# SSD state update by two 256-column vector operations instead of four of 64, and xe taken from the transposed x in PSUM

## The chip, the cores and the metric

The kernel runs on one core of a Trainium2 chip. The metric is the device time of one execution in microseconds (us), as the median of several runs. The core has five engines with a queue each: TensorE (PE, with its weight loads shown as PEld), VectorE (DVE), ScalarE (ACT), GpSimd (POOL) and SyncE (SP), which here issues the transfers. Each queue is worked off in order; an instruction that waits for a semaphore holds what stands behind it on its engine.

## The reference

One layer of a decoder trunk: a Mamba-2 SSD branch and an attention branch read the same normalised input, are projected, gated, merged and added to the residual. Only the SSD branch matters here. For 16 heads of 64 columns, in two groups of 8 heads that share B and C (state size 64), in 8 chunks of 128 tokens:

```python
xdt = xs.astype(jnp.float32) * dt[..., None]
...
a_cs = jnp.cumsum(ac, axis=-1)
...
decay_states = jnp.exp(a_cs[..., -1:] - a_cs)
states = jnp.einsum("bclgn,bgrcl,bclgrp->bcgrpn", bc, decay_states, xc)
...
new_states = jnp.einsum("bgrzc,bcgrpn->bzgrpn", decay_chunk, states)
...
y_off = jnp.einsum("bclgn,bcgrpn,bgrcl->bclgrp", cc, prev_states, jnp.exp(a_cs))
y = (y_diag + y_off).reshape(bsz, s, g, r, p) + d_skip...
```

So the state after a chunk is the state before it, times one decay per head, plus B^T (decay_states * dt * x). The kernel runs this as a recurrence over the chunks.

## The kernel before, in words

All large products are made of a high and a low part in a reduced-precision fp32 (`split`, L97 to L100: ACT copies the high part, DVE subtracts to get the low part; all such copies stand at L98 and all such subtractions at L99, and are told apart by their tiles).

Up to about 490 us the kernel computes the input projections. In that part `ssm_sums` (L401) makes, once for all heads and chunks, the 128x128 tables `acs` (cumulated a), `dec` (decay_states, by an exponential on ACT at L418) and `ed` (the decay of a whole chunk per head, 64 rows for each of the two groups, L420 and L421); `dt` was made before it.

From about 495 to 723 us runs the SSD stage. The loop at L764 goes over four quads of heads (`qd`, four heads or 256 columns each); each quad is done in two halves of four chunks by `ssd_half` (L678). Quads 0 and 1 belong to group 0 and keep their state `st32` in partitions 0 to 63, quads 2 and 3 belong to group 1 and keep it in partitions 64 to 127. For one chunk:

- `ab` is loaded by SP (L688), made into the decay matrix on ACT (L690, L692), multiplied with `cb` on DVE (L693) and split into `m4` (m in the profile).
- PE transposes x into the PSUM tile `xps` (L698; `xp` in the profile), of which there is one buffer. DVE makes xd = x * dt (L707) from it, then xe = xd * dec (L710), both 128x256, and both are split into `xr`. Chunk 7 makes no xe.
- PE forms the state's addition `sps` (L718, three products) from the split xe. DVE brings `st32` up to date in four operations of 64 columns, one per head (L724), each st * ed + sps with ed as a scalar per partition. That is done in chunks 1 to 6 of each quad, 24 times in all; chunk 0 only copies (L720). The new state is split into `sn` on ACT and DVE (L728), with the low part in the other half of the partitions.
- PE forms `yd` (L735) and, from the previous state, `yo` (L746, L747); DVE puts them together into `ys` (L748 on 128 partitions, L751 twice on 64, for the lower and then the upper half).

Between the quads stand other projections as filling for PE (`FILL`: three value slabs by `t_slab`, L136 to L138, and seven q or k slabs by `c_slab`, L111 to L113). A scheduler in the build sets the order of the instructions on each engine; `ssd_half` gets a higher priority than the filling. After the last quad the squares `sacc` are summed by PE (L791) and DVE reads the sum (L794); the attention stage begins behind that, since it takes over the memory of this stage.

Of the kernel before, what the change touches and what calls it, by code (L numbers as in the profile page):

```python
# [27 lines left out]
ALU = mybir.AluOpType  # L28
# [37 lines left out]
def build(ctx, tc, t):  # L66
    nc = tc.nc
    V, A, G, PE, SP = nc.vector, nc.scalar, nc.gpsimd, nc.tensor, nc.sync
# [10 lines left out]
    def ev(name):  # L79
        return evp.tile([P, 1028], F32, tag="ev", bufs=4, name=name)  # L80
# [119 lines left out]
    with tc.tile_pool(name="st", bufs=1, side="right") as st, \  # L200
# [29 lines left out]
        for g in range(4, 8):  # L230
# [10 lines left out]
                        op0=ALU.mult)  # L241
        V.tensor_scalar(out=cols[:, R_SCALE:R_SCALE + 8], in0=cols[:, R_SCALE:R_SCALE + 8], scalar1=1.0, scalar2=None,
                        op0=ALU.add)
# [83 lines left out]
    dt = const.tile([P, NC, SH], F32, name="dt")  # L327
    acs = const.tile([P, NC, SH], F32, name="acs")
    dec = const.tile([P, NC, SH], F32, name="dec")
    ed = const.tile([P, NC, 8], F32, name="ed")  # L330
# [29 lines left out]
    with tc.tile_pool(name="pa", bufs=1, side="right") as pa, \  # L360
# [40 lines left out]
        def ssm_sums():  # L401
            a = ev("a")
            A.activation(out=hb[:, 24:40], in_=hb[:, 24:40], func=AF.Exp)
            V.scalar_tensor_tensor(out=a[:, 0:128].rearrange("p (c h) -> p c h", h=16), in0=dt, scalar=-1.0,
                                   in1=hb[:, 24:40].rearrange("p (o n) -> p o n", o=1).broadcast_to([P, 8, 16]),
                                   op0=ALU.mult, op1=ALU.mult)
            af = a[:, 0:128]
            ps = pap.tile([P, 512], F32, tag="pp", bufs=5, name="pp")
            PE.matmul(ps[:, 0:128], lhsT=tri, rhs=af, start=True, stop=True)
            PE.matmul(ps[:, 128:256], lhsT=ones, rhs=af, start=True, stop=True)  # L410
            PE.matmul(ps[:, 256:384], lhsT=af, rhs=tri, start=True, stop=True)
            acf = acs.rearrange("p c h -> p (c h)")
            V.tensor_copy(out=acf, in_=ps[:, 0:128])
            et = a[:, 128:256]
            A.activation(out=et, in_=ps[:, 128:256], func=AF.Exp)
            dm = a[:, 256:384]
            V.tensor_tensor(out=dm, in0=ps[:, 128:256], in1=acf, op=ALU.subtract)
            A.activation(out=dec.rearrange("p c h -> p (c h)"), in_=dm, func=AF.Exp)  # L418
            ev3 = et.rearrange("p (c h) -> p c h", h=16)
            V.tensor_copy(out=ed[0:64], in_=ev3[0:64, :, 0:8])  # L420
            V.tensor_copy(out=ed[64:128], in_=ev3[64:128, :, 8:16])  # L421
            at_ = a[:, 384:512]
            V.tensor_copy(out=at_, in_=ps[:, 256:384])
            SP.dma_start(out=a_scr, in_=at_)
            ea = a[:, 512:640]
            A.activation(out=ea, in_=ps[:, 256:384], func=AF.Exp)
            SP.dma_start(out=e_scr, in_=ea)
# [209 lines left out]
    with tc.tile_pool(name="sd", bufs=1, side="right") as sd, \  # L637
            tc.tile_pool(name="sdp", bufs=1, space=PSUM) as sdp:

        def sp():  # L640
            return sdp.tile([P, 512], F32, tag="sp", bufs=4, name="sp")
# [36 lines left out]
        def ssd_half(qd, hf, xs, ys, st32, sn):  # L678

            g = qd // 2  # L680
            gs = slice(g * 64, (g + 1) * 64)
            for c in range(4 * hf, 4 * hf + 4):
# [13 lines left out]
                xps = sdp.tile([P, 512], F32, tag="xp", bufs=1, name="xp")  # L696
# [4 lines left out]
                def h4(ap):  # L701
                    return ap.rearrange("p (h d) -> p h d", h=4)

                def hb4(src):
                    return src[:, c, 4 * qd:4 * qd + 4].rearrange("p (h o) -> p h o", o=1).broadcast_to([P, 4, 64])
                xd = sd.tile([P, 256], F32, tag="xd", bufs=2, name="xd")
                V.tensor_tensor(out=h4(xd), in0=h4(xps[:, 0:256]), in1=hb4(dt), op=ALU.mult)  # L707
                if c < NC - 1:
                    xe = sd.tile([P, 256], F32, tag="xe", bufs=2, name="xe")
                    V.tensor_tensor(out=h4(xe), in0=h4(xd), in1=hb4(dec), op=ALU.mult)  # L710
                    split(xe, xr[:, 2], xr[:, 3], 256)
                split(xd, xr[:, 0], xr[:, 1], 256, V)

# [1 line left out]
                if c < NC - 1:  # L715
                    sps = sp()
                    for n, (x, y) in enumerate(((0, 2), (1, 2), (0, 3))):
                        PE.matmul(sps[:, 0:256], lhsT=bt[:, c, x, :], rhs=xr[:, y, :], start=(n == 0), stop=(n == 2))  # L718
                    if c == 0:
                        V.tensor_copy(out=st32[gs], in_=sps[gs, 0:256])  # L720
                    else:
                        for i in range(4):
                            hq = slice(i * 64, (i + 1) * 64)
                            V.scalar_tensor_tensor(out=st32[gs, hq], in0=st32[gs, hq],  # L724
                                                   scalar=ed[gs, c, 4 * (qd % 2) + i:4 * (qd % 2) + i + 1],
                                                   in1=sps[gs, hq], op0=ALU.mult, op1=ALU.add)
                    sn = sd.tile([P, 256], F32R, tag="sn", bufs=2, name="sn")
                    split(st32[gs], sn[gs], sn[half[1 - g]], 256)  # L728

                yd = sp()  # L730
                for i in range(4):
                    o = yd[0:64, (i % 2) * 256 + (i // 2) * P:(i % 2) * 256 + (i // 2) * P + P]
# [4 lines left out]
                if c > 0:  # L737
# [6 lines left out]
                    for i in range(2):  # L744
# [4 lines left out]
                                    op=ALU.mult)  # L749
# [14 lines left out]
        for qd in range(4):  # L764
            st32, sn = sd.tile([P, 256], F32, tag="st32", bufs=1, name="st32"), None
# [487 lines left out]
```

## Time and profile before

| | |
|---|---|
| median of 3 runs | 1218.62 us (1217.94 to 1220.36) |
| the profiled execution's own time | 1224.31 us |
| its span in the trace | 1222.6 us |
| mean granted TensorE clock | 0.988 |
| busy share of the span: PE, PEld, DVE, ACT, POOL | 95%, 80%, 78%, 52%, 7% |
| DVE instructions | 1946 |
| SSD stage | about 495 to 723 us |

A busy share counts the time in which at least one instruction of the engine runs. Instructions of an engine overlap: a matmul's record lasts longer than the distance to the start of the next one, and so does many a vector operation's. What one more instruction costs is therefore the distance from start to start, and not the duration of its record. A wait row names who waited for whom, with total, number of times and the longest.

### The profile page before, as it was taken

How to read it: one execution, taken by the hardware profiler on the slowest of the kernel's cores; microseconds unless marked ns; L12 is line 12 of the kernel's file. 1: busy time of each engine (PE TensorE's matmuls, PEld its weight loads, DVE VectorE, ACT ScalarE, POOL GpSimd, SP SyncE). 2: the span in 40 equal slices, each digit the busy share in tenths (PEclk: the TensorE clock that was granted, in tenths of full speed). 3: DMA queues.
4: the chain of work that ended last, by engine and by line, in shares of the span. 5: the costliest groups of instructions: out<-in, count | busy, mean ns of one | idle time of the engine just before them, and what ended most of it. 6: DMA issues, size and time to landing. Idle time of an engine off the chain costs nothing.

```text
span 1222.6 us, 18382 instructions
## 1 busy us (share of the span) xinstructions
PE 1165.0 (95%) x6206; PEld 981.2 (80%) x6206; DVE 955.9 (78%) x1946; ACT 635.5 (52%) x1260; POOL 88.4 (7%) x152
## 2 busy tenths in 40 slices
PE   3999999999999999999999989999988999999997
PEld 2788888788877877998887778888877887788876
DVE  5856699788987784589999986664677977989967
ACT  7554443454443334776676633454456554454465
POOL 1000000000000000000000012222322220000001
PEclk9999999999999999999999989999998999999999
DMA  9665643655485676546545668422246526875334
GB/s 370 263 243 166 218 138 100 207 204 176 156 290 171 218 239 201 186 152 222 186 154 178 207 216 286 144 94 81 87 165 203 175 88 228 283 241 181 109 95 147
DMA packets 109018, 228.26 MB, mean 187 GB/s; under 512 B 12362, under 2 KB 20220, under 8 KB 107900
## 3 DMA queue, kind: packets, MB, share of 16 engines
q1 hardware_dynamic: 108924, 227.09, 55.2%
q8 instruction: 49, 0.80, 0.3%
q14 instruction: 45, 0.37, 0.1%
HBM read 159.14 MB, written 67.90 MB: 186 GB/s over the span
## 4 chain that ended last, share of the span: by engine, by line
PE 62%; DVE 16%; DMA 13%; ACT 4%; issue 4%; SPq 1%; POOL 0%; POOLq 0%; DVEq 0%; ACTq 0%
PE pp L497 4%; PE pv L1067 4%; PE pp L499 4%; PE pp L500 4%; PE lg L1036 3%; PE mm L497 3%; PE mm L499 3%; PE mm L500 3%; PE mm L112 3%; PE mm L113 3%; PE mm L111 3%; PE tp L1057 2%; DMA ab<-a_scr 2%; DMA wr<-w_c 2%; PE mm L919 2%
## 5 line engine op out<-in xcount | busy, mean ns | idle before, releaser
L98 ACT CAST wh<-wr 128x512 fp32r<-128x512 f32 (+1 forms) x214 | 131.0, 620 | 176.2 <-DMA wr<-w_c 32.4
L99 DVE TENSOR_TENSOR wl<-wr,wh 128x512 fp32r<-128x512 f32 (+1 forms) x214 | 146.9, 693 | 44.0 <-ACT wh L98 43.3
L112 PE MATMUL mm<-hl,wh 128*128 128x512 f32 x288 | 116.7, 405 | 0.4 <-DVE hl L306 0.4
L111 PE MATMUL mm<-hh,wh 128*128 128x512 f32 x288 | 116.2, 408 | 0.0
L113 PE MATMUL mm<-hh,wl 128*128 128x512 f32 x288 | 115.5, 402 | 0.0
L136 PE MATMUL mm<-wh,hh 128*128 128x256 f32 (+1 forms) x256 | 73.7, 289 | 1.9 <-DVE tmp L348 1.9
L137 PE MATMUL mm<-wl,hh 128*128 128x256 f32 (+1 forms) x256 | 74.4, 291 | 0.0
L138 PE MATMUL mm<-wh,hl 128*128 128x256 f32 (+1 forms) x256 | 73.7, 289 | 0.0
L1042 ACT ACTIVATE pr<-pr,sm 128x1024 f32<-128x1024 f32 (+3 forms) x64 | 49.9, 780 | 42.4 <-DVE sm L1041 35.1
L1060 ACT CAST pth<-tp 128x512 fp32r<-128x512 f32 (+1 forms) x80 | 42.4, 543 | 47.7 <-PE tp L1057 39.5
L1037 DVE CUSTOM_DVE_ANT_0 pr<-lg,fb 128x512 f32<-128x512 f32 (+1 forms) x96 | 51.4, 552 | 17.0 <-PE lg L1036 12.4
L112 PEld LDWEIGHTS mm<-hl,wh 128*128 128x128 f32 x288 | 55.2, 192 | 11.0 <-DVE hl L306 1.0
L113 PEld LDWEIGHTS mm<-hh,wl 128*128 128x128 f32 x288 | 55.0, 191 | 10.4
L111 PEld LDWEIGHTS mm<-hh,wh 128*128 128x128 f32 x288 | 54.7, 193 | 10.2 <-ACT hh L305 0.3
L690 ACT ACTIVATE ab<-ab,acs 128x128 f32<-128x128 f32 x128 | 41.2, 391 | 40.7 <-DMA ab<-a_scr 40.5
L1045 POOL TENSOR_SCALAR pr<-pr,sm 128x1024 f32<-128x1024 f32 (+3 forms) x64 | 51.8, 811 | 87.5 <-DVE sm L1044 70.2
L1061 DVE TENSOR_TENSOR ptl<-tp,pth 128x512 fp32r<-128x512 f32 (+1 forms) x80 | 50.0, 632 | 10.3 <-ACT pth L1060 10.2
L98 ACT CAST sh<-sr 128x512 fp32r<-128x512 f32 x57 | 34.0, 619 | 43.8 <-DVE sr L479 32.4
L796 POOL TENSOR_TENSOR fl<-fl,mhalf 128x8 f32<-128x8 f32 x1 | 1.6, 1647 | 698.2 <-DVE fl L794 698.2
L136 PEld LDWEIGHTS mm<-wh,hh 128*128 128x128 f32 x256 | 48.8, 191 | 2.4 <-DVE tmp L348 2.2
L1067 PE MATMUL pv<-pth,vh 128*128 128x256 f32 (+1 forms) x160 | 45.8, 287 | 4.5 <-DVE zg L1070 3.8
L138 PEld LDWEIGHTS mm<-wh,hl 128*128 128x128 f32 x256 | 49.1, 192 | 0.0
(407 smaller groups left out, 3509.8 us busy)
## 6 DMA issues: line engine op xcount, KB each, us to landing
wr<-w_c SPq DMA_DIRECT2D x116, 256.0 KB, 3.9
wa<-w_ada SPq DMA_DIRECT2D x8, 1024.0 KB, 11.4
g_scr<-gt SPq DMA_DIRECT2D x16, 512.0 KB, 4.2
ab<-a_scr SPq DMA_DIRECT2D x32, 256.0 KB, 3.9
gt<-g_scr SPq DMA_DIRECT2D x32, 256.0 KB, 3.7
wr<-w_ps SPq DMA_DIRECT2D x28, 256.0 KB, 2.6
wr<-w_pa SPq DMA_DIRECT2D x28, 256.0 KB, 2.8
wr<-so SPq DMA_DIRECT2D x28, 256.0 KB, 2.7
```

What stands on the lines that cost most here:

```text
L98: A.copy(out=hi[:, :n], in_=raw[:, :n])
L99: eng.tensor_tensor(out=lo[:, :n], in0=raw[:, :n], in1=f32(hi[:, :n]), op=ALU.subtract)
L111: PE.matmul(ps, lhsT=hi[:, cs], rhs=xh[k][:, hs], start=(k == 0), stop=False)
L112: PE.matmul(ps, lhsT=hi[:, cs], rhs=xl[k][:, hs], start=False, stop=False)
L113: PE.matmul(ps, lhsT=lo[:, cs], rhs=xh[k][:, hs], start=False, stop=(k == 7))
L136: PE.matmul(o, lhsT=xh[k][:, ts], rhs=hi[:, cs], start=(k == 0), stop=False)
L137: PE.matmul(o, lhsT=xh[k][:, ts], rhs=lo[:, cs], start=False, stop=False)
L138: PE.matmul(o, lhsT=xl[k][:, ts], rhs=hi[:, cs], start=False, stop=(k == 7))
L497: PE.matmul(ps, lhsT=f[0][:, w], rhs=xh[:, hs], start=(first and k == 0), stop=False, skip_group_check=True)
L499: PE.matmul(ps, lhsT=f[0][:, w], rhs=xl[:, hs], start=False, stop=False, skip_group_check=True)
L500: PE.matmul(ps, lhsT=f[1][:, w], rhs=xh[:, hs], start=False, stop=(k == 3), skip_group_check=True)
L1067: PE.matmul(pv[:, o0:256], lhsT=x[kb // 4][:, kb % 4, vs], rhs=y[:, d:d + m], start=(kb == 0 and i == 0), stop=(kb == 2 * qq + 1 and i == 2))
```

## The change

`ssm_sums` multiplies `dec` by `dt` once (one more 128x128 operation on DVE, between projections). xe is then x * (dec * dt), read from `xps`, and not from xd. The state is multiplied in place by its four decays in one operation of 256 columns, with `ed` broadcast over the 64 columns of each head, and `sps` is added in a second one. The lines behind the first insertion move by one, so that xd stands at L708, xe at L711, the multiplication at L724 and the addition at L726; from L727 on the numbers are those of before.

```diff
             A.activation(out=dec.rearrange("p c h -> p (c h)"), in_=dm, func=AF.Exp)
+            V.tensor_tensor(out=dec, in0=dec, in1=dt, op=ALU.mult)
...
                 if c < NC - 1:
                     xe = sd.tile([P, 256], F32, tag="xe", bufs=2, name="xe")
-                    V.tensor_tensor(out=h4(xe), in0=h4(xd), in1=hb4(dec), op=ALU.mult)
+                    V.tensor_tensor(out=h4(xe), in0=h4(xps[:, 0:256]), in1=hb4(dec), op=ALU.mult)
                     split(xe, xr[:, 2], xr[:, 3], 256)
...
-                        for i in range(4):
-                            hq = slice(i * 64, (i + 1) * 64)
-                            V.scalar_tensor_tensor(out=st32[gs, hq], in0=st32[gs, hq],
-                                                   scalar=ed[gs, c, 4 * (qd % 2) + i:4 * (qd % 2) + i + 1],
-                                                   in1=sps[gs, hq], op0=ALU.mult, op1=ALU.add)
+                        eh = ed[gs, c, 4 * (qd % 2):4 * (qd % 2) + 4].rearrange("p (h o) -> p h o", o=1)
+                        V.tensor_tensor(out=h4(st32[gs]), in0=h4(st32[gs]), in1=eh.broadcast_to([64, 4, 64]),
+                                        op=ALU.mult)
+                        V.tensor_tensor(out=st32[gs], in0=sps[gs, 0:256], in1=st32[gs], op=ALU.add)
```

The scheduler lays the queues of the SSD stage anew. On DVE at the start of quad 0, from the copy of chunk 0's state on (st is the state, sn its split, xr the split of xe and xd, m the split of the decay matrix), the order before is:

```order
L720 COPY st_4650<-sp 64x256
L99 TENSOR_TENSOR sn<-st_4650,sn 64x256
L724 SCALAR_TENSOR_TENSOR st_4650<-st_4650,ed,sp 64x64 x4
L99 TENSOR_TENSOR xr<-xe,xr 128x256
L99 TENSOR_TENSOR xr<-xd,xr 128x256
L99 TENSOR_TENSOR m_4818<-ab,m_4818 128x512
L707 TENSOR_TENSOR xd<-xp,dt 128x256
L748 TENSOR_TENSOR ys<-sp,eb 128x2x128
L710 TENSOR_TENSOR xe<-xd,dec 128x256
```

At the same place of the changed kernel stands:

```order
L721 COPY st_4651<-sp 64x256
L99 TENSOR_TENSOR sn<-st_4651,sn 64x256
L724 TENSOR_TENSOR st_4651<-st_4651,ed 64x256
L99 TENSOR_TENSOR xr<-xe,xr 128x256
L726 TENSOR_TENSOR st_4651<-sp,st_4651 64x256
L99 TENSOR_TENSOR xr<-xd,xr 128x256
L99 TENSOR_TENSOR m_4815<-ab,m_4815 128x512
L708 TENSOR_TENSOR xd<-xp,dt 128x256
L711 TENSOR_TENSOR xe<-xp,dec 128x256
```

Multiplication and addition are parted by another operation, and xe stands right behind xd. In quad 2, whose state lies in partitions 64 to 127, the order on DVE around the update of chunk 2 is, before:

```order
L707 TENSOR_TENSOR xd<-xp,dt 128x256
L693 TENSOR_TENSOR ab<-ab,cb_4548 128x512
L724 SCALAR_TENSOR_TENSOR st_6056<-st_6056,ed,sp 64x64
L99 TENSOR_TENSOR xr<-xe,xr 128x256
L724 SCALAR_TENSOR_TENSOR st_6056<-st_6056,ed,sp 64x64 x3
L99 TENSOR_TENSOR xr<-xd,xr 128x256
L710 TENSOR_TENSOR xe<-xd,dec 128x256
```

And now, around the update of the same chunk:

```order
L724 TENSOR_TENSOR st_6033<-st_6033,ed 64x256
L708 TENSOR_TENSOR xd<-xp,dt 128x256
L711 TENSOR_TENSOR xe<-xp,dec 128x256
L694 TENSOR_TENSOR ab<-ab,cb_4549 128x512
L99 TENSOR_TENSOR xr<-xe,xr 128x256
L99 TENSOR_TENSOR xr<-xd,xr 128x256
L726 TENSOR_TENSOR st_6033<-sp,st_6033 64x256
L99 TENSOR_TENSOR m_6328<-ab,m_6328 128x512
```

The multiplication has moved ahead of five operations on all partitions, and the addition behind them. Over the whole stage xe follows xd directly in 25 of 28 chunks, against 2 of 28 before, and multiplication and addition are neighbours in 3 of 24 updates. Ahead of the stage only the new operation is added; behind it a few instructions change places.

## The prediction

> **What bounds the kernel now.** I read the busy shares first, then the busy time by stretches for the SSD stage, the groups of instructions by shape there, the timeline of DVE around single updates, the waits, and the chain that ended last.
>
> Busy time by stretches; the columns are start to end, length, then busy us (with instructions) of PE, PEld, DVE, ACT, POOL, the granted clock, the DMA share and GB/s:
>
> ```profile
> 495.00:520.00 25.00, 23.56 (x203) 23.35 (x202) 13.34 (x35) 19.18 (x48) 0.00 (x0) 1.00 0.49 164
> 520.00:612.00 92.00, 91.64 (x727) 84.27 (x727) 85.29 (x215) 65.72 (x171) 0.00 (x0) 1.00 0.59 186
> 612.00:720.00 108.00, 103.16 (x701) 88.13 (x700) 100.84 (x237) 66.06 (x159) 0.00 (x0) 1.00 0.56 179
> ```
>
> From 520 to 720 us DVE is busy 85.3 + 100.8 = 186.1 of 200 us and idle for 13.9. PE is busy almost throughout, but its records overlap, so that says less. Pieces of the chain that ended last, with start and length:
>
> ```profile
> 553.12 0.76 DVE st L724 x4
> ...
> 658.17 4.69 DMA ab<-a_scr
> ...
> 689.68 0.90 DVE st L724 x4
> ...
> 694.37 0.61 PE sp L718 x3
> ...
> 723.23 0.80 PE sp L791 x8
> ```
>
> From 535 to 694 us most of its pieces are of DVE, and between them stand loads of `ab`, which SP issues once DVE has freed a buffer; from 694 to 723 us they are matmuls. So a microsecond less on DVE should count up to 694, and nothing behind that: at the end DVE waits for PE:
>
> ```profile
> 720.32 1.48 DVE L785 TENSOR_TENSOR sacc<-sacc,zt 128x512 f32<-128x512 f32 x2
> 724.05 0.17 DVE L794 TENSOR_SCALAR fl<-sp 128x8 f32<-128x8 f32 x1 [2.25 <-PE sp L791]
> ```
>
> **Part 1, the state update.** The groups by shape in this stage (mean ns of one behind the busy time):
>
> ```profile
> L724 DVE SCALAR_TENSOR_TENSOR st<-st,ed,sp 64x64 f32<-64x64 f32 x96 | 21.1, 279 | 0.8 <-PE sp L718 0.4
> L710 DVE TENSOR_TENSOR xe<-xd,dec 128x256 f32<-128x256 f32 x28 | 11.7, 418 | 0.2
> L751 DVE TENSOR_TENSOR ys<-sp,ys 64x256 f32<-64x256 f32 x56 | 23.2, 415 | 0.7
> ```
>
> Removed are 96 operations of 0.279 us, 26.8 us of records. Added are 48 of 64x256. The multiplication has two operands in SBUF, one of them broadcast, as L710 has; the addition reads PSUM and SBUF as L751 does; so 48 x 0.418 = 20.1 us. The records shrink by 6.7 us. But the 96 keep DVE busy for only 21.1 us: they overlap. The timeline shows by how much; first an update in quad 0:
>
> ```profile
> 558.64 0.42 DVE L707 TENSOR_TENSOR xd<-xp,dt 128x256 f32<-128x256 f32 x1
> 558.97 0.84 DVE L751 TENSOR_TENSOR ys<-sp,ys 64x256 f32<-64x256 f32 x2
> 559.85 0.85 DVE L724 SCALAR_TENSOR_TENSOR st<-st,ed,sp 64x64 f32<-64x64 f32 x4
> 560.62 0.68 DVE L693 TENSOR_TENSOR ab<-ab,cb 128x512 f32<-128x512 f32 x1
> 561.22 0.41 DVE L710 TENSOR_TENSOR xe<-xd,dec 128x256 f32<-128x256 f32 x1
> 561.55 0.41 DVE L99 TENSOR_TENSOR xr<-xe,xr 128x256 fp32r<-128x256 f32 x1
> ```
>
> then two in quad 2:
>
> ```profile
> 641.93 0.90 DVE L724 SCALAR_TENSOR_TENSOR st<-st,ed,sp 64x64 f32<-64x64 f32 x4
> 642.86 0.43 DVE L710 TENSOR_TENSOR xe<-xd,dec 128x256 f32<-128x256 f32 x1
> 643.20 0.42 DVE L99 TENSOR_TENSOR xr<-xe,xr 128x256 fp32r<-128x256 f32 x1
> ...
> 646.43 0.90 DVE L724 SCALAR_TENSOR_TENSOR st<-st,ed,sp 64x64 f32<-64x64 f32 x4
> 647.36 0.85 DVE L751 TENSOR_TENSOR ys<-sp,ys 64x256 f32<-64x256 f32 x2
> 648.24 1.41 DVE L779 SCALAR_TENSOR_TENSOR ys<-xs,dskip,ys 128x512 f32<-128x512 f32 x2
> ```
>
> In quad 0 the four take 0.77 us until the next starts, which begins 0.08 before they end. In quad 2, where the state lies in partitions 64 to 127, they take 0.93, and the next begins 0.03 after the end. The same with L751, whose second half goes to partitions 64 to 127: 0.03 of a gap behind it. Between operations that start at the same partition the overlap is 0.08 to 0.09 (561.22 to 561.55: 0.41 long, next after 0.33; 558.64 to 558.97: 0.42 long, next after 0.33), taken as 0.085. So a change of the start partition costs 0.085 + 0.025 = 0.11 us. [...]
>
> For the two new operations this means: in quads 0 and 1, 2 x 0.335 = 0.67 against 0.77, a gain of 0.10 in each of 12 updates. In quads 2 and 3 four operations in a row had two changes of partition; multiplication and addition with other work between them have four, so 0.93 + 0.11 = 1.04 stands against up to 2 x (0.45 + 0.11) = 1.12, a loss of up to 0.08, less where a neighbour changes the partition anyway. For the sum I counted, along the order from the first xd to L794, the operations whose operands start at other partitions than those of the one ahead, or that wait for the one ahead: 147 of 486 before, 157 of 438 now. So 339 overlap before and 281 now: the 58 fewer overlaps give back 58 x 0.085 = 4.9 us, the ten more gaps 10 x 0.025 = 0.25. DVE's net: -6.7 + 4.9 + 0.25 = **-1.6 us**, nearly all of it in quads 0 and 1. [...] This is a quarter of what the records suggest.
>
> **Part 2, xe from PSUM.** L707 reads `xps` from PSUM and L710 reads xd from SBUF, both 128x256:
>
> ```profile
> L707 DVE TENSOR_TENSOR xd<-xp,dt 128x256 f32<-128x256 f32 x32 | 13.5, 421 | 8.5 <-PE xp L698 8.0
> ```
>
> 421 against 418 ns: 28 x 0.003 = 0.1 us more, taken as 0. [...] What changes is that `xps` is free only after xe, 0.335 us after xd, and the next transposes wait for that on PE, with the filling queued behind them. So far they waited four times:
>
> ```profile
> PEld xp L698 <- DVE xd L707: 1.5, 2, 0.9
> PE xp L698 <- DVE xd L707: 0.9, 2, 0.5
> ```
>
> If the same four wait on, 4 x 0.335 = 1.3 us of PE's waiting is added; the bounds are 0 and 28 x 0.335 = 9.4. I take 0 for the end of the stage: these few waits lie in the stretch where DVE ends the chain, and PE catches up.
>
> **Part 3, dec * dt.** One operation of 128x128, once. L417 is the same form, and behind the place where it goes DVE waits for a transfer:
>
> ```profile
> 217.33 0.29 DVE L417 TENSOR_TENSOR a<-pp,acs 128x128 f32<-128x128 f32 x1 [0.34 <-ACT a L415]
> ...
> 218.25 0.06 DVE L536 MEMSET xp<- 128x3 f32 x1
> 219.97 0.69 DVE L587 TENSOR_TENSOR sr<-wr 128x512 f32<-128x512 f32 x1 [1.66 <-DMA wr<-w_pa]
> ```
>
> 0.29 us in a pause of 1.66: nothing. Without the pause it would cost at most 0.3.
>
> **Part 4, the new order.** ACT's and DVE's waits around the state:
>
> ```profile
> ACT ab L690 <- DMA ab<-a_scr: 40.5, 22, 4.1
> ACT sn L98 <- DVE st L724: 13.6, 5, 5.4
> DVE sn L99 <- ACT sn L98: 2.1, 3, 1.1
> ```
>
> The multiplication needs no matmul and can go ahead, so that after `sps` only one operation of 0.42 stands before the new state. Against that the multiplication still takes its place in the same queue. What the new order does to the waits for `ab` and to DVE's 13.9 us of idle time no row shows. I bound it by a third of that idle time on either side, 4.6 us, and take 0, since nothing in the order favours a side: of 28 low parts of sn, 5 now stand at most three rows behind the state, against 3.
>
> Sum: -1.6 + 0 + 0 + 0. The profiled execution took 1224.31 us (span 1222.6, 1.7 around it) and would take 1222.7. That is 5.7 above the median of the runs, 1218.62; the terms are absolute and small, so I carry them over: **1217.0 us**.
>
> **The rivals.**
>
> - *The gain stays on DVE* (0.16): PE with its filling is the real bound of the whole stage. For it: the last 29 us of the chain are PE, and DVE waits 2.25 us at the end. Against it: PEld is busy for 88.1 of the last 108 us, so PE has gaps. Time: 1218.6.
> - *The short way from the products to the state counts* (0.22). With 24 updates whose four operations take 0.77 to 0.93, L724's full length is 20.4 us; the addition alone takes 0.335 to 0.45, so up to 11 us leave the way to the new state. If half of that, 5.5, shows: 1213.1. For it: ACT waits 13.6 us for the state. Against it: only five of those waits exist, and PE, which needs the state a chunk later, scarcely waits for it.
> - *The transposes wait for xe* (0.23), the one that ends on the other side. Place: L698 at the head of PE's queue, one buffer of `xps`. Price: 0.335 us for each chunk in which PE stands there already. For it: xe now directly follows xd, so PE's moment, which the scheduler put behind xd, is exactly there. Against it: only four waits so far. It outweighs the gain by 0.2% from (1.6 + 2.4) / 0.335 = 12 chunks on; at 14 of 28 it is 4.7 - 1.6 = +3.1, so 1221.7.
> [...]
>
> **How the numbers follow.** The forecast has 0.36. About 0.2%, 2.4 us, is what a measurement of this kernel can tell from no change. The forecast itself lies inside this; with the uncertainty of part 4 I put 0.11 of its 0.36 beyond 2.4 us of gain and 0.25 inside. Faster: 0.22 + 0.11 = 0.33. Same: 0.25 + 0.16 + 0.03 = 0.44. Slower: 0.23. The forecast's own range is 1214.5 to 1218.6; the range over the cases reaches to both outer rivals, 1213.0 to 1222.2.
>
> **What would show it.** Right: DVE's records in the stage shrink by about 6.7 us while the stage gets shorter by only 1 to 2; almost all of it in quads 0 and 1 (up to the copy of quad 2's state); in quads 2 and 3 a multiplication or an addition begins 0.02 to 0.03 after the end of the one ahead, and does not overlap; xe lasts 0.42. Wrong: waits of L698 for L711 of more than 4 us in all; xe of 0.48 us; a stage that is 4 us or more shorter, with ACT's wait for the state gone; or operations at partitions 64 to 127 that overlap with their neighbours.

## The result, and the profile after

| | before | after |
|---|---|---|
| median | 1219.49 us (1217.94 to 1221.01, 4 runs) | 1235.19 us (1231.12 to 1236.85, 4 runs) |
| the profiled execution's own time, span | 1224.31, 1222.6 us | 1231.12, 1229.4 us |
| mean granted TensorE clock | 0.988 | 0.987 |

The ratio is 1.0118 (95% interval 1.0095 to 1.0141): the changed kernel is 1.2% slower, where 0.1% faster was forecast, and it lies outside the range of 1213.0 to 1222.2 us. The trace of the changed kernel is of the fastest of its executions, and that of before is of one slower than its four runs, so that the traces lie 6.8 us apart and the medians 15.7.

The work on DVE did become less. These are the groups of operations of the changed kernel by shape in the SSD stage; behind the bar stand busy time and mean ns of one, then the idle time before them:

```profile
L711 DVE TENSOR_TENSOR xe<-xp,dec 128x256 f32<-128x256 f32 x28 | 11.6, 412 | 0.1
L726 DVE TENSOR_TENSOR st<-sp,st 64x256 f32<-64x256 f32 x24 | 10.0, 418 | 0.5
L724 DVE TENSOR_TENSOR st<-st,ed 64x256 f32<-64x256 f32 x24 | 10.0, 417 | 0.5
```

The update's records are 24 x (0.417 + 0.418) = 20.0 us in the place of 26.8. But DVE did not get further with it. The busy time by stretches (length, then PE, PEld, DVE, ACT, POOL with their instructions):

```profile
520.00:612.00 92.00, 87.29 (x673) 78.93 (x671) 77.97 (x176) 61.06 (x158) 0.00 (x0) 1.00 0.57 173
612.00:720.00 108.00, 98.87 (x691) 85.55 (x691) 97.50 (x210) 66.02 (x163) 0.00 (x0) 1.00 0.55 175
```

From 520 to 720 us DVE is busy for 78.0 + 97.5 = 175.5 us and idle for 24.5; before it was idle for 13.9. PE (186.2 us against 194.8), ACT (127.1 against 131.8) and the weight loads (164.5 against 172.4) are all less busy too, at the same granted clock of 1.00: no engine became the bound, all of them wait more. Where the time is lost shows on the timeline of DVE, first of before, near the start of the stage (fourth chunk of quad 0):

```profile
515.32 0.69 DVE L693 TENSOR_TENSOR ab<-ab,cb 128x512 f32<-128x512 f32 x1 [2.25 <-ACT ab L692]
```

and then of the changed kernel, at the same place and at the end of the stage:

```profile
511.76 0.69 DVE L694 TENSOR_TENSOR ab<-ab,cb 128x512 f32<-128x512 f32 x1 [1.91 <-ACT ab L693]
...
730.77 0.17 DVE L794 TENSOR_SCALAR fl<-sp 128x8 f32<-128x8 f32 x1 [2.38 <-PE sp L791]
```

In the changed kernel the fourth chunk comes 3.6 us earlier and L794 6.7 us later (it stood at 724.05). The earlier start is within the scatter of single traces: the first xd starts at 504.3 us before and at 500.9 in the changed kernel, and at 502.4 to 504.8 in five kernels of the experiments that have the changed kernel's operations ahead of the stage. From that fourth multiplication of `ab` to L794, before and then after:

```profile
515.32:724.05 208.73, 203.50 (x1487) 180.40 (x1485) 191.98 (x464) 135.68 (x338) 0.00 (x0) 1.00 0.57 180
```

```profile
511.76:730.77 219.01, 204.81 (x1489) 181.42 (x1487) 189.98 (x416) 134.90 (x338) 0.00 (x0) 1.00 0.55 171
```

For the same part of the work the changed kernel takes 10.3 us longer. DVE works 2.0 us less in it and is idle for 29.0 us, against 16.8. The waits of the changed kernel between 495 and 735 us (total, times, longest):

```profile
ACT ab L691 <- DMA ab<-a_scr: 46.9, 19, 5.2
DVE ab L694 <- ACT ab L693: 13.8, 9, 2.9
```

and DVE's wait for the same thing before:

```profile
DVE ab L693 <- ACT ab L692: 4.5, 3, 2.2
```

DVE's waits for `ab` grew by 9.3 us. In the chain of work that ended last, between 495 and 735 us, the loads of `ab` hold 23.1% now against 11.4% before. First the line of before, then of the changed kernel:

```profile
by line: DMA ab<-a_scr 11.4%; issue 6.6%; DVE m L99 5.5%; ACT ab L690 4.6%; DVE xr L99 4.6%; DVE st L724 4.4%; DVE ys L751 4.3%; DVE ab L693 3.8%; DVE wl L99 3.7%; DMA xs<-x_scr 3.2%; DVE ys L779 3.0%; PE mm L111 3.0%; PE mm L112 2.9%; PE m
```

```profile
by line: DMA ab<-a_scr 23.1%; ACT ab L691 9.0%; issue 6.8%; DVE m L99 4.6%; DMA xs<-x_scr 3.9%; DVE xr L99 3.5%; ACT xr L98 3.0%; DVE ys L751 2.9%; PE mm L137 2.5%; ACT ab L693 2.4%; PE mm L136 2.4%; PE mm L138 2.4%; DVE ys L780 2.2%; DVE s
```

How one such wait comes about is seen from the split of m that frees a buffer of `ab` (there are three) to the multiplication that needs its next content, three chunks on. DVE, SP (a row with SPq is an issue of a transfer), ACT and DVE again in the changed kernel:

```profile
552.88 0.68 DVE L99 TENSOR_TENSOR m<-ab,m 128x512 fp32r<-128x512 f32 x1
```

```profile
554.10 0.33 SPq L350 DMA_DIRECT2D v_scr<-vt  x1
554.51 0.38 SPq L689 DMA_DIRECT2D ab<-a_scr  x1
```

```profile
559.96 1.28 ACT L691 ACTIVATE ab<-ab,acs 128x128 f32<-128x128 f32 x4 [4.54 <-DMA ab<-a_scr]
...
561.62 0.62 ACT L693 ACTIVATE ab<-ab 128x512 f32<-128x512 f32 x1
```

```profile
562.27 0.69 DVE L694 TENSOR_TENSOR ab<-ab,cb 128x512 f32<-128x512 f32 x1 [2.95 <-ACT ab L693]
```

The buffer is free at 553.56. SP issues the load 0.95 us later, since a store stands ahead of it; this is the longest such delay in the changed kernel, and the mean of its 29 loads is 0.10 us. ACT can begin 5.45 us after that and needs 2.3 more, and DVE, which has only 13 operations of other work in between, is there 2.95 us too early. Over the stage 14.9 operations stand between such a split and the multiplication three chunks on, in the mean of 29; before it were 18.7, and the new operations in the old order would have 16.9. Four short operations count as four there; in time, DVE works 6.5 us in the mean between the two, and 7.5 before. This way round is called the ring below. The traces suggest it as the cause; they do not show whether it is one.

### The profile page after: what moved, and what is told of

Its sections match the earlier page's. It is cut to its first block, busy times and chain, and to the rows that moved or that the text cites. A ratio compares the mean times of both kernels' runs of the same rounds, so it can differ in the third digit from the quotient of the medians.

```text
span 1229.4 us, 18345 instructions
## 1 busy us (share of the span) xinstructions
PE 1163.4 (95%) x6206; PEld 979.5 (80%) x6206; DVE 953.2 (78%) x1899; ACT 634.2 (52%) x1260; POOL 87.9 (7%) x152
## 4 chain that ended last, share of the span: by engine, by line
PE 64%; DMA 13%; DVE 12%; ACT 6%; issue 4%; SPq 1%; POOL 0%; POOLq 0%; DVEq 0%; ACTq 0%
PE pp L498 5%; DMA ab<-a_scr 5%; PE pp L500 5%; PE pp L501 5%; PE pv L1067 4%; PE mm L498 4%; PE mm L500 4%; PE mm L501 4%; PE lg L1036 3%; PE mm L112 3%; PE mm L111 3%; PE mm L113 3%; PE tp L1057 2%; ACT ab L691 2%; PE mm L919 2%
## 5 line engine op out<-in xcount | busy, mean ns | idle before, releaser
L137 PEld LDWEIGHTS mm<-wl,hh 128*128 128x128 f32 x256 | 49.0, 192 | 0.2
## 6 DMA issues: line engine op xcount, KB each, us to landing
wa<-w_ada SPq DMA_DIRECT2D x8, 1024.0 KB, 11.4
```

Of the source, the lines that this page charges most:

```text
L137: PE.matmul(o, lhsT=xh[k][:, ts], rhs=lo[:, cs], start=False, stop=False)
```

## The experiments

In the experiments a kernel can be given the order of another. To that end every instruction of an engine is made to follow the one ahead of it in a table, with no semaphore, so that nothing is left to the scheduler:

```python
for a, b in zip(order[:-1], order[1:]):
    tc.add_manual_dep(rows[e][b], rows[e][a].name, no_sync, reason="pin")
```

"Old" is the order of before, "new" that of the changed kernel. A ratio is to the kernel before on the same chip, with its 95% interval. Where operations differ between the kernels, the multiplication stands at the place of the first of the four old operations and the addition at that of the last; four old operations in the new order stand at the addition's place; xe stands directly behind xd. In the edits, `ORDERS` stands in words for the tables. No kernel was pinned to its own order with nothing else changed; the nearest one, further down, measured 1.0011, so the pinning itself seems to cost little.

### The operations or their order

Theory A was that the redrawn order of the queues costs the time, B that the transposes wait because xe now holds `xps`, C that the new operations are dearer than their rows say. Four kernels tell them apart.

**Only xe** (dec * dt, and xe from `xps`), in the order that the scheduler gives it:

```diff
+            V.tensor_tensor(out=dec, in0=dec, in1=dt, op=ALU.mult)
...
-                    V.tensor_tensor(out=h4(xe), in0=h4(xd), in1=hb4(dec), op=ALU.mult)
+                    V.tensor_tensor(out=h4(xe), in0=h4(xps[:, 0:256]), in1=hb4(dec), op=ALU.mult)
```

> Only dec * dt and xe from PSUM; the state update stays in four operations; the scheduler lays the queues itself. Theory A (the redrawn order of the queues costs the time, above all by late loads of ab, and the operations themselves cost nothing): no fixed sign, since this edit alone is a third draw of the order; DVE's waits for ab follow the time. Theory B (xps is held until xe is read, and the next transposes wait): slower by about 10 us or more, with over 4 us of PE waiting for xe in the waits. Theory C (the two new state operations cost it): no change.

Measured: 1.0085 (1.0065 to 1.0105), 1234.08 us. PE's waits for xe are 1.5 us, and not over 4 as B asked for.

**Only the state update**, in the scheduler's own order:

```diff
-                        for i in range(4):
...
-                            V.scalar_tensor_tensor(out=st32[gs, hq], ...)
+                        eh = ...
+                        V.tensor_tensor(out=h4(st32[gs]), in0=h4(st32[gs]), in1=eh.broadcast_to([64, 4, 64]), op=ALU.mult)
+                        V.tensor_tensor(out=st32[gs], in0=sps[gs, 0:256], in1=st32[gs], op=ALU.add)
```

> Only the state update by two operations of 256 columns; xe still from xd; the scheduler lays the queues itself. Theory A: again no fixed sign, a draw of its own. Theory B: no change. Theory C: slower by about 15 us.

Measured: 1.0072 (1.0050 to 1.0093), 1231.85 us. Each half of the change draws an order of its own, and each costs most of a per cent. DVE's waits for `ab` are 10.2 us with only xe and 8.0 with only the state update, between 4.5 before and 13.8 with both, so they follow the time as A has it.

**All new operations, old order:**

```diff
         build(ctx, tc, t)
+        pin(tc, nc)
+ORDERS = {PE: old, DVE: old, ACT: old, SP: old}
```

> All operations of the change, but every instruction of PE, DVE, ACT and SP pinned to the order of the kernel before: the multiplication where the first of the four stood, the addition where the last stood, xe directly behind xd. Theory A: 1216 to 1220 us, DVE 1 to 2 us less work in the stage, the ab waits as before. Theories B and C: about 1235.

Measured: 1.0018 (1.0002 to 1.0033), 1226.75 us. The small gain that A expected from the operations is not there.

**Old operations, new order:**

```diff
         build(ctx, tc, t)
+        pin(tc, nc)
+ORDERS = {PE: new, DVE: new, ACT: new, SP: new}
```

> The operations of the kernel before (four updates of 64 columns, xe from xd, no dec * dt), pinned to the order of the changed kernel: the four updates where the addition stands, xe directly behind xd. Theory A: about 1235 us, perhaps 1 to 3 more, with DVE's idle time in the stage above 20 us. Theories B and C: about 1219.

Measured: 1.0125 (1.0107 to 1.0143), 1238.60 us.

The busy time from 520 to 720 us (PE, PEld, DVE, ACT) of the new operations in the old order, and then of the old operations in the new order:

```profile
520.00:720.00 200.00, 191.01 (x1407) 169.03 (x1406) 180.60 (x396) 130.60 (x326) 0.00 (x0) 1.00 0.58 181
```

```profile
520.00:720.00 200.00, 185.01 (x1339) 164.25 (x1338) 172.44 (x419) 128.43 (x323) 0.00 (x0) 0.98 0.55 169
```

In the old order DVE is idle for 200 - 180.6 = 19.4 us, in the new one for 27.6, with the old operations (and a granted clock of 0.98). The order alone costs 1.25%, the operations alone 0.2%: A holds, B and C fall. All three orders that the scheduler drew for an edited kernel were slower than the one that it drew for the kernel before.

### Which part of the order

Theory A1 was the place of the loads of `ab` in SP's queue, A2 the order on DVE, A3 that on PE or ACT. The new operations were run with some queues in the old order.

```diff
+ORDERS = {PE: new, DVE: new, ACT: new, SP: old}
```

> The changed kernel's operations, with its order on PE, DVE and ACT, but with the order on SP (the transfers) of before. The order as a whole was worth 0.8% between the new operations in the new order (1235.2 us) and in the old one (1226.8), with a chip-to-chip scatter of some 3 us. Theory A1 (the loads of ab stand at a worse place in SP's queue, behind loads of eb and stores that wait longer, so that ACT waits for them): SP's order is most of it, so the ratio to before falls from 1.012 to 1.002 to 1.005, and DVE's waits for ab fall from 13.8 to about 5 us. Theory A2 (the order on DVE): ratio stays at 1.010 to 1.013. Theory A3 (PE or ACT): the same, 1.010 to 1.013.

Measured: 1.0135 (1.0114 to 1.0156).

```diff
+ORDERS = {PE: new, DVE: old, ACT: new, SP: old}
```

> The changed kernel's operations, with its order on PE and ACT, and the order of before on SP and DVE (multiplication and addition at the places of the first and last of the four operations, xe directly behind xd). A1: as the kernel with SP's old order alone, 1.002 to 1.005. A2: 1.002 to 1.005 here, 1.010 or more with SP's old order alone. A3 (PE's order, with its filling, or ACT's): still 1.008 to 1.013.

Measured: 1.0261 (1.0234 to 1.0288).

```diff
+ORDERS = {PE: old, DVE: old, ACT: new, SP: old}
```

> The changed kernel's operations, in the order of before on PE, DVE and SP, and only ACT's queue in the new order. A1 and A2: within 0.2% of the kernel that has the old order everywhere (1.002). A3 on ACT: 1.006 or more; A3 on PE: 1.002 here and 1.008 or more with the new order on PE and ACT.

Measured: 1.0228 (1.0204 to 1.0251).

With SP's old queue alone the kernel costs as much as with the whole new order, within the intervals, so A1 finds nothing there. The two mixtures with DVE's old order are worse than either whole order: with ACT's new queue among old ones the kernel loses 2.3%, more than twice what the whole new order costs. So this order cannot be taken apart by engines; its queues fit each other, and no share of the loss belongs to one of them. Nor is the loss of these mixtures that of the changed kernel: with ACT's queue alone in the new order, DVE waits 12.1 us for ACT's copies of sn and 10.1 us for those of m, against 2.1 and 0.9 before, and 9.1 us for `ab`. From 520 to 720 us the granted clock is 0.94 in the two kernels with ACT's new and DVE's old order, against 1.00 before; whether that is a cause or a consequence is not shown. The three runs decide nothing between A2 and A3. A1 was tested by itself as well, with the loads on a queue of their own:

```diff
-                SP.dma_start(out=ab, in_=a_scr[r0:r0 + 4]...)
+                G.dma_start(out=ab, in_=a_scr[r0:r0 + 4]...)
+ORDERS = {PE: new, DVE: new, ACT: new, SP: new without these loads}
```

> The changed kernel, order as it is, but the 32 loads of ab are issued by POOL, which is idle in this stage, and not by SP. A load then starts as soon as its buffer is free, and nothing in SP's queue stands ahead of it. A1: DVE's waits for ab fall from 13.8 us to under 5, ACT's waits for the load from 46.9 to under 30, and the time falls by 0.5 to 1% to a ratio of 1.002 to 1.006. A2 and A3: ACT's waits for the load may fall, but the time stays within 0.3% of the changed kernel (1.009 to 1.013).

Measured: 1.0131 (1.0110 to 1.0152): nothing came back, and A1 alone falls. Its waits show why:

```profile
POOL ab L689 <- DVE m L99: 171.0, 26, 13.1
ACT ab L691 <- DMA ab<-a_scr: 51.1, 18, 5.3
...
DVE ab L694 <- ACT ab L693: 16.3, 10, 3.1
```

With a queue to themselves, 26 of the loads wait for DVE's split of m, since no buffer is free. SP's queue had not held them up in the changed kernel either: there 28 of 29 loads start within 0.5 us of the end of the split that frees their buffer. That led to theory A4, the ring of the three buffers, against A5, that the order costs through many couplings of which `ab` is only the place where it shows.

### Without the loads, and with the ring moved

**The new operations without the loads of `ab`**, first in the new order, then in the old one:

```diff
-                SP.dma_start(out=ab, in_=a_scr[r0:r0 + 4]...)
                 for i in range(4):
-                    A.activation(out=ab[:, i, :], in_=ab[:, i, :], func=AF.Relu, scale=-1.0,
+                    A.activation(out=ab[:, i, :], in_=tri, func=AF.Relu, scale=-1.0,
+ORDERS = {PE: new, DVE: new, ACT: new, SP: new without these loads}
```

> The changed kernel, each queue in its order, with the 32 loads of ab left out: the first operation on ab on ACT reads a constant table of the same size in the place of the loaded one, so that the decay matrix is not the right one. Buffers, waits for buffers and all other work stay. Theory A4 (the ring of three ab buffers: DVE's split of chunk c frees the buffer, the load of chunk c + 3 takes 4.4 us, ACT 2.3, and where the new order puts fewer DVE operations between than that takes, DVE waits): the ring is 4.4 us shorter, DVE's waits for ab fall from 13.8 to under 4 us, and with the old order's counterpart beside it the order is worth less than 0.3%. Theory A5 (the order costs through many couplings, of which ab is only the place where it shows): the order stays worth 0.6% or more.

Measured: 0.9932 (0.9908 to 0.9955), 1216.51 us.

```diff
+ORDERS = {PE: old, DVE: old, ACT: old, SP: old without these loads}
```

> The new operations in the old order (1.0018 with the loads), with the 32 loads of ab left out in the same way. A4: DVE waits for ab little there already, so it gains 0.2 to 0.6% (ratio 0.996 to 1.000), and the kernel in the new order without the loads lies within 0.3% of it. A5: the two lie 0.6% or more apart.

Measured: 0.9915 (0.9890 to 0.9940), 1214.41 us. Without the loads the two orders lie 0.17% apart, inside the intervals of both, against 1.0% with them (1.0118 and 1.0018). The old order gained 1.0%, more than the 0.2 to 0.6% that A4 had for it. From the fourth multiplication of `ab` to L794 the two traces take 202.4 and 202.5 us. The new order without the loads, by its chain of work and by stretches:

```profile
by line: PE mm L137 7.5%; PE mm L138 7.4%; PE mm L136 7.3%; PE mm L112 5.8%; PE mm L113 5.8%; PE mm L111 5.7%; PE sp L734 4.8%; issue 4.7%; DMA ut<-u_scr 3.3%; DVE xr L99 2.6%; DVE ab L693 2.3%; DVE wl L99 2.2%; PE sp L718 2.2%; DVE m L99 2
```

```profile
520.00:720.00 200.00, 195.66 (x1436) 175.55 (x1436) 188.60 (x409) 136.97 (x333) 2.43 (x2) 0.99 0.47 155
```

PE's matmuls now lead the chain, and DVE is idle for 11.4 us and not 24.5. So without the loads the order costs next to nothing. By itself this does not exclude other couplings: the traffic of the loads is missing as well (DMA share 0.47, against 0.57 and 0.55 in the two stretches of the changed kernel), and a smaller cost could hide behind PE. The kernel with both edits at once, further down, keeps the loads.

**The old order with the new ring:** only the 32 multiplications of `ab` and the 32 splits of m on DVE stand at their new places.

```diff
+ORDERS = {PE: old, DVE: old but ab L694 and m L99 at their new places, ACT: old, SP: old}
```

> The new operations in the old order on every engine (1.0018), except for 64 operations on DVE: the 32 multiplications of ab by cb and the 32 splits of the decay matrix stand at the places that they have in the changed kernel's queue. So the DVE operations between the split that frees a buffer and the multiplication three chunks on are 14.9 in the mean, as in the changed kernel, and not 16.9. A4: DVE's waits for ab rise from 5 to 10 us or more, and the time by 0.5 to 1% (ratio 1.007 to 1.012). A5: less than 0.3% (1.000 to 1.005).

Measured: 1.0242 (1.0215 to 1.0269). More than A4 asked for, so by itself it may only be one more mixture that does not fit. Its control moves as many other operations about as far:

```diff
+ORDERS = {PE: old, DVE: old but xd L708 and xe L711 at their new places, ACT: old, SP: old}
```

> Control for the transplanted ring (1.0242): the new operations in the old order, except for the 60 operations that make xd and xe, which stand at the places that they have in the changed kernel's queue on DVE. 54 of them move, by 2.2 places in the mean; of the 64 operations of the ring 49 moved, by 2.9. Between split and multiplication stand 16.8 operations, as in the old order. A4: within 0.5% of the old order (1.000 to 1.007). A5: 1.015 or more.

Measured: 1.0057 (1.0039 to 1.0075). This mixture costs 0.4% over the old order, and the ring 2.2%. The ring is the sensitive part; how much of the 2.2% is misfit, one control doesn't tell.

**Only the state update, in the old order.** This takes the forecast's term by itself.

```diff
-                        for i in range(4):
...
+                        eh = ...
+                        V.tensor_tensor(out=h4(st32[gs]), in0=h4(st32[gs]), in1=eh.broadcast_to([64, 4, 64]), op=ALU.mult)
+                        V.tensor_tensor(out=st32[gs], in0=sps[gs, 0:256], in1=st32[gs], op=ALU.add)
+ORDERS = {PE: old, DVE: old, ACT: old, SP: old}
```

> The kernel before, in its own order on every engine, with only the state update changed: the multiplication stands at the place of the first of the four operations, the addition at that of the last; xe is still made from xd at its old place. By the count of overlaps the two operations are worth -1.6 us, nearly all of it in quads 0 and 1: ratio 0.9987 (0.997 to 1.000). All new operations in the old order measured 1.0018. If that came from xe (behind xd, reading xps, whose release moves back), this kernel is at 0.998 to 1.000; if it came from the state update, it is at 1.001 to 1.003.

Measured: 1.0003 (0.9984 to 1.0021). The interval holds both 0.9987 and no change, and a good part of what was expected if the loss came from the state update. It does not settle where the 0.18% of all new operations in the old order comes from.

### The buffer earlier

If the ring holds the stage, a buffer that is free earlier must help. In the traces the split of m stands 1.6 to 1.8 us behind the copy on ACT that it needs, in the mean, behind other work of DVE. It was moved up by as many operations as had started after that copy's end.

**Old operations, old order, splits up:**

```diff
+ORDERS = {PE: old, DVE: old with each m L99 0 to 10 places further up, ACT: old, SP: old}
```

> The kernel before, its operations and its order on every engine, but the 32 splits of the decay matrix on DVE (which free a buffer of ab) stand 0 to 10 operations further up in DVE's queue, 3.3 in the mean: each behind the last operation that started before its copy on ACT was done, so by the trace it waits for nothing new. A buffer is free 1.6 us earlier in the mean. Theory A4 (the ring of the ab buffers): ACT's waits for the loads fall from 40.5 to under 30 us, and the time falls by 0.2 to 0.8% (0.992 to 0.998). Theory A5 (an order that has been fitted costs when anything in it is moved): 1.003 or more.

Measured: 1.0011 (0.9996 to 1.0027).

**New operations, old order, splits up:**

```diff
+ORDERS = {PE: old, DVE: old, new operations, with each m L99 0 to 10 places further up, ACT: old, SP: old}
```

> The new operations in the old order (1.0018), with the 32 splits moved up in the same way by its own trace (3.1 operations in the mean): 19.9 operations of DVE then stand between the split that frees a buffer and the multiplication three chunks on, against 16.9. A4: 0.992 to 0.998. A5: 1.005 or more.

Measured: 1.0037 (1.0021 to 1.0054).

**The changed kernel, splits up:**

```diff
+ORDERS = {PE: new, DVE: new with each m L99 0 to 8 places further up, ACT: new, SP: new}
```

> The changed kernel in its own order, with the 32 splits moved up in the same way by its own trace (3.3 operations in the mean): 18.4 operations in between, against 14.9. A4: DVE's waits for ab fall from 13.8 to 7 us or less and the time by 0.5 to 1.2%, to 1.000 to 1.007. A5: 1.010 or more.

Measured: 1.0135 (1.0111 to 1.0160). None became faster: A4, as it was put, falls. The first two are also below what A5 asked for. Why the move did nothing can be read in the last of the three. First DVE, then SP:

```profile
663.84 0.69 DVE L99 TENSOR_TENSOR m<-ab,m 128x512 fp32r<-128x512 f32 x1 [0.41 <-ACT m L98]
```

```profile
665.72 0.32 SPq L777 DMA_DIRECT2D zt<-z_scr  x1
666.32 0.33 SPq L85 DMA_DIRECT2D wr<-w_c  x1
668.50 0.32 SPq L777 DMA_DIRECT2D zt<-z_scr  x1
668.91 1.25 SPq L689 DMA_DIRECT2D ab<-a_scr  x1
```

The buffer is free at 664.53, but the load starts at 668.91, behind three other transfers. In the changed kernel itself the same load stood right behind its split. DVE and SP there:

```profile
663.50 0.68 DVE L99 TENSOR_TENSOR m<-ab,m 128x512 fp32r<-128x512 f32 x1
```

```profile
663.60 0.32 SPq L777 DMA_DIRECT2D zt<-z_scr  x1
664.21 0.32 SPq L689 DMA_DIRECT2D ab<-a_scr  x1
```

There it starts 0.03 us behind the end of the split. From the timeline of all 29 such loads, start less end of the split: 0.17 us in the mean before and 0.10 in the changed kernel, and with the splits moved up 1.07 (old operations) and 1.16 (changed kernel), with 11 and 13 loads later by more than 1 us. The splits now begin 0.4 us behind their copies, 1.2 us sooner with the old operations and 1.4 us in the changed kernel; SP's queue takes back 0.9 and 1.1 us of that.

### Both at once

So theory A6: the loads stand behind two locks in a row, the buffer and SP's queue, and each hides the other. Against it stood A7: the loads cost through something else, such as ACT's place in its own order.

```diff
-                SP.dma_start(out=ab, in_=a_scr[r0:r0 + 4]...)
+                G.dma_start(out=ab, in_=a_scr[r0:r0 + 4]...)
+ORDERS = {PE: new, DVE: new with each m L99 0 to 7 places further up, ACT: new, SP: new without these loads}
```

> The changed kernel in its own order, with both changes of earlier kernels at once: the loads of ab issued by POOL (alone 1.0131), and the splits that free the buffers 3.3 operations further up in DVE's queue (alone 1.0135). Theory A6 (two locks in a row, the buffer and SP's queue): only with both does a load start earlier; ACT's waits for the loads fall from 47 to 51 us to under 35, DVE's for ab from 11 to 16 us to under 7, and the time to 1.002 to 1.008. Theory A7 (the loads cost through ACT's place in its own order, which reaches the first operation on ab too soon whatever the load does, or through something not found): 1.010 or more.

Measured: 1.0010 (0.9994 to 1.0027), 1225.66 us. By stretches, and by its waits:

```profile
520.00:720.00 200.00, 195.08 (x1437) 173.75 (x1435) 184.05 (x406) 132.16 (x331) 15.32 (x28) 1.00 0.59 184
```

```profile
POOL ab L689 <- DVE m L99: 176.4, 27, 19.2
...
ACT ab L691 <- DMA ab<-a_scr: 33.1, 15, 4.5
...
DVE ab L694 <- ACT ab L693: 5.3, 8, 1.4
```

DVE's waits for `ab` are 5.3 us against 13.8, its idle time 16.0 against 24.5, and the loads start 0.30 us behind the split. One of the two edits alone gave 1.0131 or 1.0135, both together 1.0010: the 1.2% of the changed kernel is gone, in its own order on PE and ACT and with all its loads. So the order costs its time through the loads of `ab`: this is shown, and A6 holds; the time is even a little below the 1.002 to 1.008 that it asked for.

```diff
+ORDERS = {PE: old, DVE: old with each m L99 0 to 10 places further up, ACT: old, SP: old without these loads}
```

> The kernel before, its operations and its order, with both changes: loads of ab by POOL, splits 3.3 operations further up (alone 1.0011). A6: loads start as early as their buffer allows; 0.993 to 0.999. A7: 1.000 to 1.005, as POOL takes 0.55 us for each load.

Measured: 0.9984 (0.9969 to 1.0000), 1222.47 us. That is the fastest kernel here that does the whole computation, but by 0.16% it can't be told from no change. The old order had little to win: its loads stood 0.17 us behind their splits, and DVE waited for them for 4.5 us.

What both locks leave can be put in one number from the traces: how long DVE works between the start of a load and the multiplication that needs it, in the mean of 29. It is 7.3 us before and with the new operations in the old order, 6.4 in the changed kernel and 6.6 with the old operations in the new order. With one edit alone it is 6.2 (loads by POOL) and 6.9 (splits up), with both 7.6. In the changed kernel the load (4.3 us in the mean, over the loads whose landing is in the trace) and ACT (2.3) need 6.6 us together, as an estimate. The number does not rank every run: the state update alone in the scheduler's order has 6.5 at 1.0072, and the two kernels with ACT's new and DVE's old order have 7.4 and lose over 2% elsewhere.

A fourth buffer of `ab`, against the first lock by itself, was not tried.

## Why the prediction was wrong

**The step that failed** is part 4, the new order: "What the new order does to the waits for `ab` and to DVE's 13.9 us of idle time no row shows. I bound it by a third of that idle time on either side, 4.6 us, and take 0, since nothing in the order favours a side." The order was the whole result, and the bound was too small: with the old operations the new order costs 1.25%, some 15 us. Two things were wrong in it. A third of the idle time bounded what could be won, and there was no reason to let it bound what could be lost. And something in the order did favour a side: between the split that frees a buffer and the multiplication three chunks on, DVE works 7.5 us in the old order and 6.5 to 6.7 in the new one, whichever operations stand in it. The number of operations in between was to be had from the orders: 14.9 against 18.7, and still 14.9 against 16.9 where the state update has two operations in both. So was the chance that a new order is worse than the one that a tuned kernel has. I counted low parts of sn instead.

**What bounds the stage** was half right. The chain held loads of `ab` between DVE's pieces, and I quoted one of 4.69 us, but took them to DVE's account: "a microsecond less on DVE should count up to 694". With 11.4%, and 17.3% between 535 and 694 us, the loads were the longest line of that chain. DVE's work and the loads are a ring, and a shorter stretch of work in it leaves more of the load uncovered: DVE's waits for `ab` rose from 4.5 to 13.8 us. That less work on DVE need not count is seen from the new operations in the old order, where the stretch in the ring stayed at 7.5 us. From the fourth multiplication of `ab` to L794:

```profile
515.25:728.44 213.19, 204.16 (x1488) 180.66 (x1486) 190.75 (x417) 135.84 (x340) 0.00 (x0) 1.00 0.57 176
```

DVE works 1.2 us less than before and is idle for 5.7 us more. Its waits for `ab` rose by 0.5 us (4.5 to 5.0), those for ACT's copies of sn by 2.4 (2.1 to 4.5).

**Part 1** was right in its mechanism: the records shrank by 26.8 - 20.0 = 6.8 us (6.7 forecast). From the first xd to L794, 319 operations began before the end of the one ahead in the trace of before, and 256 in that of the changed kernel, 63 fewer (58 forecast); that gave back 5.3 us of overlap (4.9 forecast). The forecast's two workings do not agree, since 12 updates at 0.10 us gain 1.2 at most, less up to 1.0 in the other 12, and the count of overlaps gives 1.6. As work on DVE the term came out: from the fourth multiplication of `ab` to L794 DVE's busy time is less by 1.0 us (state update alone, old order), 1.2 (all new operations, old order) and 2.0 (changed kernel). In quad 2 of the changed kernel none of the update's 12 operations overlaps with the one behind it. Ten of them begin 0.03 to 0.04 us behind the end of the one ahead, and two begin 0.08 before the end of the L751 ahead. DVE there:

```profile
640.28 0.43 DVE L726 TENSOR_TENSOR st<-sp,st 64x256 f32<-64x256 f32 x1
640.74 0.69 DVE L99 TENSOR_TENSOR m<-ab,m 128x512 fp32r<-128x512 f32 x1
641.35 1.28 DVE L99 TENSOR_TENSOR wl<-wr,wh 128x512 fp32r<-128x512 f32 x2
```

The split begins 0.03 us behind the addition's end, and the operation after it 0.08 before the split's end. The term of -1.6 us did not come out as time: 1.0003 for the state update alone, where its interval would allow it, and 1.0018 (1.0002 to 1.0033) for all new operations, where it does not.

**Part 2** was right: xe takes 412 ns from PSUM, against 418 from SBUF before. The 0.03 in the sum of the chances and the "xe of 0.48 us" stand for a slower read from PSUM, which no run shows. PE's waits for xe are small too:

```profile
PE xp L699 <- DVE xe L711: 0.8, 2, 0.6
PEld xp L699 <- DVE xe L711: 0.7, 1, 0.7
```

**Part 3** was right: dec * dt takes 0.292 us and lies ahead of a wait for a transfer, so that it costs nothing; the wait is 0.64 us, against 1.66 before, and only 0.29 us of that difference can be the operation's:

```profile
217.98 0.29 DVE L419 TENSOR_TENSOR dec<-dec,dt 128x128 f32<-128x128 f32 x1
218.91 0.69 DVE L588 TENSOR_TENSOR sr<-wr 128x512 f32<-128x512 f32 x1 [0.64 <-DMA wr<-w_pa]
```

**The rivals.** "The transposes wait for xe" had the right side by luck and the wrong mechanism: it asked for 4.7 us of waits, and there were 1.5. "The short way to the state counts" did not happen: ACT's wait for the state is 12.1 us against 13.6. "The gain stays on DVE" comes nearest for the operations alone: in the old order their gain shows nowhere. No rival was made of the order, although it was the one edit whose effect I had said no row shows.

**What stays open.** The new operations in the old order are slower by 0.18%, and with the splits moved up by 0.26% (1.0037 against 1.0011). The state update alone is at 1.0003, so the larger part would be xe's, but the intervals overlap, and no run tells it apart. Nor is it shown which single operations of the new order shorten the ring.

## What to carry to other kernels

Where a scheduler lays the queues, an edit has two effects, and the second, a new draw of the order, can outweigh the first: here 1.0 to 1.25% against 0.2%. To tell them apart, run the new operations in the old order. Look in the chain for transfers that are part of a ring of buffers, and add up the work between the operation that frees a buffer and the one that needs its next content, before and after, in time rather than in operations: work that is moved out of there uncovers the transfer (here 6.4 us between load and multiplication against 7.3, and 13.8 us of DVE's waits against 4.5). And when a remedy for a late transfer does nothing, look for a second lock behind the first (the buffer behind the queue, the queue behind the buffer) before giving up the cause: here either edit alone measured 1.0131 or 1.0135, and both 1.0010.

## What the runs showed that was not expected

- Queues of two working orders did not mix well: ACT's new order among the old ones costs 2.3%, and PE and ACT's new orders with DVE and SP's old ones 2.6%, while the whole new order costs 1.0 to 1.25%.
- Loads of `ab` issued by POOL take it 0.55 us each (15.32 us for 28 in the row above) and start 0.30 us behind the release of their buffer; POOL has no other work in the stage.
- Without its 32 loads of `ab` the new order is faster by 1.8% (1.0118 to 0.9932) and the old one by 1.0%. PE's share of 95% looked full before; in the new order it is busy for 195.7 of 200 us without the loads, and for 186.2 with them.
